# Second sequence's turned row split in another order around the next row's sum, two operand copies on POOL, query tile turned behind the third keys' block

## The chip, the cores and the metric

The kernel runs on one core of a Trainium2 chip. The metric is the device time of one execution in microseconds (us). Engines are named as in the profile: PE multiplies matrices, DVE and ACT do elementwise work, POOL too but only on SBUF, and SP issues DMAs. ACT and POOL also issue DMAs from their own queues. Each engine works through its own instructions in order and waits on semaphores for the others.

## The reference

One encoder layer over two independent sequences of 512 tokens with 1024 features, all in float32:

```python
h = rms_norm(x, ln1)
q, k, v, u, g_att, g_ssm = split(h @ w_in)
y_att = windowed_attention(rms_norm(q), rms_norm(k), v, sink, bias, mask)   # blocks of 128, 3 key blocks each
y_ssm = s5_branch(u, ...)          # state-space scan both ways; y = gelu(y); y * sigmoid(y @ w_glu + b_glu)
mixed = sigmoid(g_att) * y_att + sigmoid(g_ssm) * y_ssm
x = x + mixed @ w_out
h2 = rms_norm(x, ln2)
return x + square(relu(h2 @ w_up)) @ w_down
```

## The kernel before, in words

Every large product is made of three passes. An operand is split into a high part (a cast to the matrix engine's rounded float format, usually by ACT) and a low part (the rest, a subtraction, usually by DVE). `mm3` then multiplies high by high, high by low and low by high. A 128x512 piece that comes out of anything thus costs one cast and one subtraction before it can go into the next product.

The stages run in this order: input projections mixed with the state-space scan, attention, the gated product of the state-space branch, the output projection with the second normalisation, the up projection, and the down projection. In the stretches that matter here the order of PE, ACT and DVE is written out by hand (`tc.manual_schedule`), so their queues hold instructions in program order. Buffers have tags: a new tile under a tag with one buffer waits until every reader of the old tile is done.

**Attention.** Eight steps `i` (four key heads by two sequences, the sequence inside), each with four query blocks `qb`. In one block the kernel computes the scores of the current `Unit` and finishes the previous one (`prev`): its exponentials are turned by PE (`turn`, L983), cast by ACT (`high`, L988) and subtracted by DVE (`low`, L993), for each of its two or three key blocks, and multiplied with the values (`value`, L998). In between PE projects the queries of the next step (`Tile.project`, L913). The query tile of the block before (`rows`) is normalised, turned and split (`Tile.turn`, `high`, `low`, L938 to L949). A `Unit` begins with a small copy on POOL into its column 0 (L962). The last step has no next one. PE then fills in with the first products of the gated stage (`glu_pull`). These need the state-space output `y`, loaded in eight pieces `m` during steps 6 and 7; `split_y` (L1060) casts each half of a piece on ACT at the end of a block, and its subtraction (POOL, L1063) is issued at the start of the next block, from the list `y_lows`. After the loop the last unit is finished, some products are pulled, the reciprocal of the row sums is turned by PE (`final.turn`, L1027), and more products are pulled. All pulls share one list of 96 product steps.

**Output projection.** For each row block `t` (four) and sequence `sq` (two), PE computes the row of 1024 in two halves of 24 matmuls (`out_half`, L1377). DVE adds each half to the residual row `x1`. After the second half ACT squares and sums the row (`power_of`, L1397, into the buffer with tag "xn"), POOL makes the inverse root, DVE scales (`norm_of`, L1409). Between the next row's two halves PE turns this row by eight transposes (`turn_of`, L1425).

The up projection uses a seven-product scheme for blocks of two by two, where the first sequence gives two of the blocks (`B11`, `B21`) and the second two more (`x12`, `x22`). From all four come five operands, `B22`, `T1`, `T2`, `T3`, `T4`. So the turn of a first-sequence row is followed by two splits, and the turn of a second-sequence row by five splits with four differences and two copies between them (L1417 to L1445), through one intermediate `tx` of two halves `tt`, which also has the tag "xn". In the code before, the turn and the splits are issued together, ahead of the next half row:

```python
out_half(x1s[sq], sq, t, b)
if b == halves[0] and owed:
    turn_of(*owed)
```

Then come the store of the finished row to scratch on ACT's queue (L1517), the square and the normalisation. The rows `x1` have two buffers, loaded by SP (L1387). In the last row the raw up weights (`raws`, L1468) are loaded into the buffer of the first half of the output weights, and DVE forms their sums (`up_sums`, L1477); the first up products follow before the last row's turn.

## Time and profile before

| What | us |
|---|---|
| median of 3 runs | 1457.18 |
| lowest, highest run | 1455.81, 1458.38 |
| the profiled execution's own time | 1461.76 |
| its span, first to last instruction | 1460.0 |
| mean granted clock of PE | 0.994 of full |

Times in the profile are microseconds from the span's start. A timeline row gives the start, the length (both us), the engine, the line, the operation, what it writes and reads with their shapes, how many instructions are merged into it, and in brackets the idle time before it and who ended that. PE's rows overlap, since matmuls are pipelined. A row of a table of windows gives the stretch, its length, the busy time of PE, weight loads, DVE, ACT and POOL (with instructions), the granted PE clock, the DMA share and the GB/s.

### The profile page before, as it was taken

Reading aid. Unit: us, or ns where it says so; the run is one execution under the profiler, and the core shown is the slowest. Engines: PE = TensorE matmul, PEld = TensorE weight load, DVE = VectorE, ACT = ScalarE, POOL = GpSimd, SP = SyncE. Lnnn points to the kernel's source line nnn. Section 1 sums busy time; section 2 is a strip of 40 time slices with the busy share of each in tenths; the row PEclk is TensorE's granted clock in tenths of the full one; section 3 lists DMA queues with packets and bytes.
Section 4 is the critical chain, followed back from the end, with each engine's and each line's share of the span. In section 5 each row is a group of like instructions: output and inputs, shape, how many; then the busy total and the mean of one; then the engine's idle time right before and its main releaser. Section 6 shows DMA issues by size and latency. Waiting matters only on the chain.

```text
span 1460.0 us, 22047 instructions
## 1 busy us (share of the span) xinstructions
PE 1442.5 (99%) x7997; PEld 1233.4 (84%) x7997; DVE 1095.2 (75%) x1978; ACT 762.6 (52%) x1361; POOL 243.3 (17%) x394
## 2 busy tenths in 40 slices
PE   9999999999999999999999899999999999999998
PEld 8888888889999999988887688888888888888887
DVE  7999959985458999889964478777776598475654
ACT  8688852234348878883533246445454444333332
POOL 3044452004144432362000000000000000000000
PEclk9999999999999999999999899999999999999999
DMA  7356559539642632445551335444442993454441
GB/s 294 102 176 189 163 162 328 194 106 308 220 144 71 182 107 64 138 151 189 196 181 58 112 106 197 160 148 151 147 144 107 339 334 106 158 187 147 129 130 58
DMA packets 102204, 240.23 MB, mean 165 GB/s; under 512 B 12330, under 2 KB 25130, under 8 KB 102096
## 3 DMA queue, kind: packets, MB, share of 16 engines
q1 hardware_dynamic: 62304, 139.94, 29.5%
q0 software_dynamic: 16320, 48.28, 10.1%
q10 hardware_dynamic: 23472, 50.61, 9.3%
q8 instruction: 63, 1.03, 0.3%
q14 instruction: 45, 0.37, 0.1%
HBM read 169.02 MB, written 81.82 MB: 172 GB/s over the span
## 4 chain that ended last, share of the span: by engine, by line
PE 83%; DVE 9%; issue 4%; ACT 2%; DMA 2%; POOL 1%; ACTq 0%; DVEq 0%; SPq 0%; POOLq 0%
PE bank L119 14%; PE bank L118 14%; PE bank L120 14%; PE acc L187 9%; PE acc L125 5%; PE acc L919 5%; PE po L1002 2%; PE sps L970 2%; PE sps L641 2%; PE tps L986 2%; PE sps L753 2%; DVE t L716 2%; PE acc L118 1%; PE acc L120 1%; PE acc L119 1%
## 5 line engine op out<-in xcount | busy, mean ns | idle before, releaser
L187 PE MATMUL acc<-act,c_hi 128*128 128x512 f32 x768 | 243.8, 395 | 0.0
L119 PE MATMUL bank<-b_lo,a_hi 128*128 128x512 f32 (+1 forms) x449 | 174.4, 389 | 0.0
L120 PE MATMUL bank<-b_hi,a_lo 128*128 128x512 f32 (+1 forms) x449 | 174.4, 389 | 0.0
L118 PE MATMUL bank<-b_hi,a_hi 128*128 128x512 f32 (+1 forms) x449 | 174.4, 389 | 0.0
L187 PEld LDWEIGHTS acc<-act,c_hi 128*128 128x128 f32 x768 | 142.4, 188 | 28.0 <-ACT act L316 0.9
L1654 ACT CAST a_hi<-d_a 128x1024 fp32r<-128x1024 f32 x56 | 59.0, 1054 | 178.0 <-PE bank L119 175.7
L187 PE MATMUL acc<-act,c_lo 128*128 128x512 f32 x384 | 151.4, 394 | 0.0
L118 PE MATMUL bank<-act,act 128*128 128x512 f32 x368 | 143.2, 389 | 0.0
L119 PE MATMUL bank<-act,act 128*128 128x512 f32 x368 | 143.2, 389 | 0.0
L120 PE MATMUL bank<-act,act 128*128 128x512 f32 x368 | 143.2, 389 | 0.0
L1655 DVE TENSOR_TENSOR a_lo<-d_a,a_hi 128x1024 fp32r<-128x1024 f32 x56 | 68.5, 1224 | 98.0 <-ACT a_hi L1654 98.0
L919 PE MATMUL acc<-w_hi,act 128*128 128x256 f32 x512 | 114.1, 291 | 0.1
L120 PEld LDWEIGHTS bank<-b_hi,a_lo 128*128 128x128 f32 x449 | 84.3, 188 | 17.6
L119 PEld LDWEIGHTS bank<-b_lo,a_hi 128*128 128x128 f32 x449 | 84.3, 188 | 17.4
L118 PEld LDWEIGHTS bank<-b_hi,a_hi 128*128 128x128 f32 x449 | 84.3, 188 | 17.3
L919 PEld LDWEIGHTS acc<-w_hi,act 128*128 128x128 f32 x512 | 87.0, 189 | 4.0 <-PE sps L970 0.3
L187 PEld LDWEIGHTS acc<-act,c_lo 128*128 128x128 f32 x384 | 72.2, 188 | 14.8 <-DVE c_lo L178 1.0
L118 PEld LDWEIGHTS bank<-act,act 128*128 128x128 f32 x368 | 69.1, 188 | 14.5
L119 PEld LDWEIGHTS bank<-act,act 128*128 128x128 f32 x368 | 69.1, 188 | 14.4
L120 PEld LDWEIGHTS bank<-act,act 128*128 128x128 f32 x368 | 69.1, 188 | 14.2
L125 PE MATMUL acc<-act,gc_hi 128*128 128x512 f32 x256 | 80.7, 393 | 0.0
L980 ACT ACTIVATE p<-p,nmx 128x257 f32<-128x257 f32 (+1 forms) x128 | 72.0, 563 | 16.1 <-DVE nmx L974 15.2
(358 smaller groups left out, 3439.8 us busy)
## 6 DMA issues: line engine op xcount, KB each, us to landing
d_a<-a_scr SPq DMA_DIRECT2D x56, 512.0 KB, 3.6
raws<-in_w_up_dram SPq DMA_DIRECT2D x32, 512.0 KB, 4.0
a_scr<-t ACTq DMA_DIRECT2D x64, 256.0 KB, 2.9
k<-in_w_down_dram SPq DMA_DIRECT2D x32, 512.0 KB, 6.0
c_raw<-in_w_ug_dram SPq DMA_DIRECT2D x48, 256.0 KB, 4.1
ct_scr<-ctab POOLq DMA_DIRECT2D x16, 512.0 KB, 4.4
ctab_in<-ct_scr POOLq DMA_DIRECT2D x16, 512.0 KB, 6.2
a_scr<-a ACTq DMA_DIRECT2D x32, 256.0 KB, 2.0
```

Of the source, the lines that this page charges most:

```text
L118: PE.matmul(ps, a[0], b[0], start=first, stop=False)
L119: PE.matmul(ps, a[0], b[1], start=False, stop=False)
L120: PE.matmul(ps, a[1], b[0], start=False, stop=last)
L125: PE.matmul(ps, w[wi][:, k, :], rows[yi], start=k + p == 0, stop=k == KT - 1 and p == 2)
L187: PE.matmul(ps, w[wi][:, k, :], hT[s][hi][:, k, :], start=n == 0, stop=n == 3 * KT - 1)
L641: PE.matmul(ps[:, i * P:(i + 1) * P], bm[:, ri, g, :], u_sb[:, gp * SH + g, :], start=True, stop=True)
L716: V.tensor_mul(t1, h[:, i], a8r)
L753: PE.matmul(o, ctab[:, g0 % SI + g, ri, 0:T * CH], st[:, ri, g].rearrange("p s k -> p (s k)"), start=False, stop=ri == 1)
L919: PE.matmul(self.ps, hT[sq][act][:, k, col:col + P], w[:, k % 4, :], start=i == 0, stop=i == 3 * KT - 1)
L980: S.activation(p, p, AF.Exp, bias=self.nmx[:, h:h + 1], scale=-1.0, accum_out=self.sums[:, h, self.qb:self.qb + 1])
L1654: S.copy(hi, src)
L1655: V.tensor_sub(lo, src, hi.bitcast(F32))
```

## The change

There are four edits.

1. In the output projection, `turn_of` is cut in two. The transposes stay where they were; the splits (`put_turned`) are issued behind the second half row. For the second sequence's rows, the same operations are put in another order, with independent ones side by side, and the add and the square of the row that PE has just finished (`last`) stand ahead of the last two subtractions. The store of the finished row is issued behind its normalisation. The very last row keeps the old order. The first two raw up weights are loaded one row earlier.
2. In `split_y`, the casts of piece 6 are copies on POOL, issued directly ahead of its subtractions.
3. From the seventh attention step on (`i` above 5), the third key block of the previous unit is turned and split ahead of the query tile.
4. Behind the last unit 13 products are pulled instead of 10.

```diff
         def split_y(m, half):
-            S.copy(hi, lo.bitcast(F32))
-            return lambda: GP.tensor_tensor(lo, lo.bitcast(F32), hi.bitcast(F32), op=ALU.subtract)
+            def low():
+                if m == 6:
+                    GP.tensor_copy(hi, lo.bitcast(F32))
+                GP.tensor_tensor(lo, lo.bitcast(F32), hi.bitcast(F32), op=ALU.subtract)
+            if m != 6:
+                S.copy(hi, lo.bitcast(F32))
+            return low
...
                     cur.largest(3)
+                    if n3 > 2 and i > 5:
+                        prev.turn(2)
                     if rows:
                         rows.turn()
-                    if n3 > 2:
+                    if n3 > 2 and i < 6:
                         prev.turn(2)
...
                     project(4)
+                    if n3 > 2 and i > 5:
+                        prev.high(2)
+                        prev.low(2)
                     if rows:
                         rows.high()
                         rows.low()
-                    if n3 > 2:
+                    if n3 > 2 and i < 6:
                         prev.high(2)
                         prev.low(2)
...
-            glu_pull(10)
+            glu_pull(13)
             gate_out(1)
             final.invert()
             final.turn()
...
+        def put_turned(sq, t, last=lambda: None, between=()):
...
             if sq == 0:
                 xb.reverse()
                 put(B11, xb[0])
                 put(B21, xb[1])
+                last()
                 return
             tx = rn2.tile([P, 2, 4, P], F32, tag="xn", name="tx", bufs=1)
             tt = [tx[:, 0], tx[:, 1]]
             x11, x21, x12, x22 = xb
+            if not between:
+                S.copy(tt[0], x11)
+                high(B22, x22)
+                V.tensor_sub(tt[0], x12, tt[0])
+                low(B22, x22)
+                high(T1, tt[0])
+                V.tensor_sub(tt[1], x22, tt[0])
+                low(T1, tt[0])
+                high(T2, tt[1])
+                S.copy(tt[0], x22)
+                low(T2, tt[1])
+                V.tensor_sub(tt[0], tt[0], x12)
+                high(T3, tt[0])
+                V.tensor_sub(tt[1], tt[1], x21)
+                high(T4, tt[1])
+                last()
+                low(T3, tt[0])
+                low(T4, tt[1])
+                xb.clear()
+                return
...
         for t in range(NT // 2):
+            if t == 1:
+                w_first = [load_part(0, i) for i in range(2)]
...
             for sq in range(NSEQ):
-                halves = (0, 1) if t else (1,)
-                for b in halves:
...
-                    out_half(x1s[sq], sq, t, b)
-                    if b == halves[0] and owed:
-                        turn_of(*owed)
-                if t == 3 and sq == 1:
+                x1, tail = x1s[sq], (sq, t) == (1, 3)
+                if t:
+                    out_half(x1, sq, t, 0)()
+                    turn_of(*owed)
+                    if tail:
+                        put_turned(*owed[:2])
...
+                add = out_half(x1, sq, t, 1)
+                scaled = []
+
+                def add_and_square():
+                    add()
+                    scaled.extend(power_of(x1))
+
+                if t and not tail:
+                    put_turned(*owed[:2], last=add_and_square)
+                else:
+                    add_and_square()
+                if tail:
                     break
-                S.dma_start(x1_scr[rows_of(sq, t), :], x1s[sq])
-                owed = sq, t, norm_of(x1s[sq], *power_of(x1s[sq]))
-        scaled = power_of(x1s[1])
+                if owed and not t:
+                    turn_of(*owed)
+                    put_turned(*owed[:2])
+                owed = sq, t, norm_of(x1, *scaled)
+                S.dma_start(x1_scr[rows_of(sq, t), :], x1)
...
-        turn_of(1, 3, xn, [lambda: None, lows[0], lambda: next(second), lows[1]])
+        turn_of(1, 3, xn)
+        put_turned(1, 3, between=[lambda: None, lows[0], lambda: next(second), lows[1]])
```

`out_half` now returns its add as a function to be called later; the other helpers are unchanged.

## The prediction

> **What bounds the kernel now.** I read the page's busy line first, then the table of who waited for whom, limited to the matrix engine, then the timeline around its longest waits, then the windows there for the granted clock.

> ```profile
> PE 1442.5 (99%) x7997; PEld 1233.4 (84%) x7997; DVE 1095.2 (75%) x1978; ACT 762.6 (52%) x1361; POOL 243.3 (17%) x394
> ...
> PE tps L1425 <- DVE rn_xn L1409: 9.0, 3, 3.0
> PE po L1002 <- ACT ph L990: 1.2, 3, 0.8
> ...
> PE tps L1027 <- DVE rsum L1022: 0.4, 1, 0.4
> ```

> PE sets the end almost everywhere, so only an instant at which PE stands still can be won. The change removes no matmul. The waits (total, times, longest) name three places, and the change touches all three. The large one is three waits of 3.0 us for a normalised row at the turning transposes (L1425), in the output-projection stage.

> ```profile
> 763.45 1.03 PE L1425 MATMUL sps<-ident,rn_xn 128*128 128x128 f32 x8
> ...
> 764.56 0.40 PE L119 MATMUL acc<-act,act 128*128 128x512 f32 x1
> ...
> 774.99 0.39 PE L120 MATMUL acc<-act,act 128*128 128x512 f32 x1
> 778.38 1.94 PE L1425 MATMUL tps<-ident,rn_xn 128*128 128x128 f32 x8 [3.00 <-DVE rn_xn L1409]
> ...
> 793.02 1.04 PE L1425 MATMUL sps<-ident,rn_xn 128*128 128x128 f32 x8
> ...
> 821.43 1.03 PE L1425 MATMUL sps<-ident,rn_xn 128*128 128x128 f32 x8
> ...
> 853.72 1.04 PE L1425 MATMUL sps<-ident,rn_xn 128*128 128x128 f32 x8
> ```

> A wait costs more than its 3.0 us. From 764.56 to 774.99 lie 46 matmul steps: 10.43/46 = 0.2267 us each. One turn costs 764.56 - 0.23 - 763.45 = 0.88. Between the second sequence's turns at 763.45 and 793.02 PE has four half rows of 24 matmuls and two turns: 96 x 0.2267 + 2 x 0.88 = 23.53. It took 29.57, so 6.04 are lost. From 793.02 to 821.43 the work is the same and 28.41 - 23.53 = 4.88 are lost. From 821.43 to 853.72 there are 108 matmuls (three half rows and 36 of the first up products), 26.25 us of work, so 6.04 are lost again. **Sum 16.96 us**, of which the standing still is 778.38 - (774.99 + 0.23) = 3.16 each, 9.48. The rest is the clock:

> ```profile
> 778.00:779.00 1.00, 0.62 (x3) 0.65 (x4) 0.84 (x2) 0.00 (x0) 0.00 (x0) 0.50 0.00 0
> ...
> 784.00:785.00 1.00, 1.00 (x5) 0.84 (x4) 0.00 (x0) 0.00 (x0) 0.00 (x0) 0.85 0.00 0
> ...
> 645.00:650.00 5.00, 4.25 (x22) 3.18 (x21) 3.05 (x7) 4.68 (x13) 5.00 (x5) 1.00 0.40 105
> ```

> The column after POOL's is the granted clock: 0.50 when PE resumes, 0.85 only in the stretch from 784. The short wait at 646 (below) leaves it at 1.00.

> **The row order, step by step.** Why is the row late? The first sequence's row is added, squared and normalised only after the second sequence's whole five-part split:

> ```profile
> 764.58 0.59 ACT L1417 CAST act<-sps 128x512 fp32r<-128x512 f32 x1 [4.27 <-PE sps L1425]
> ...
> 765.06 0.59 ACT L1437 COPY tx<-tps 128x512 f32<-128x512 f32 x1
> ...
> 765.80 0.68 DVE L1438 TENSOR_TENSOR tx<-sps,tx 128x512 f32<-128x512 f32 x1
> ...
> 766.52 0.62 ACT L1417 CAST act<-tx 128x512 fp32r<-128x512 f32 x1 [0.87 <-DVE tx L1438]
> ...
> 767.17 0.69 DVE L1419 TENSOR_TENSOR act<-tx,act 128x512 fp32r<-128x512 f32 x1 [0.69 <-ACT act L1417]
> ...
> 773.11 0.69 DVE L1419 TENSOR_TENSOR t<-tx,t 128x512 fp32r<-128x512 f32 x1 [0.69 <-ACT t L1417]
> 773.72 0.68 DVE L1383 TENSOR_TENSOR x<-acc,x 128x512 f32<-128x512 f32 x1
> 774.43 0.33 ACTq L1517 DMA_DIRECT2D x_scr<-x  x1
> 774.81 1.06 ACT L1400 ACTIVATE rn_xn<-x 128x1024 f32<-128x1024 f32 x1 [1.73 <-DVE x L1383]
> ...
> 776.95 1.28 DVE L1409 SCALAR_TENSOR_TENSOR rn_xn<-x,rs,ln_bc 128x1024 f32<-128x1024 f32 x1 [2.55 <-POOL rs L1403]
> ```

> The split runs from 764.58 to the add at 773.72 because each part waits on the one before, alternating between ACT and DVE. The hops, start to start: ACT to DVE 0.65 (766.52 to 767.17), DVE to ACT 0.72 (765.80 to 766.52), DVE to DVE 0.61 (773.11 to 773.72), ACT to ACT 0.48 (764.58 to 765.06). The new order issues the same seven ACT and nine DVE operations, with the independent ones in between. Walked with these hops from 764.58 = 0: ACT copy 0, ACT B22 0.48; DVE x12 difference 0.65, B22 rest 1.26; ACT T1 1.37; DVE x22 difference 1.87, T1 rest 2.48; ACT T2 2.59, ACT copy (it overwrites what the T1 rest reads) 3.20; DVE T2 rest 3.24, difference 3.85, last difference 4.46; ACT T3 4.57, T4 5.18. The add is free at 5.07 but waits for its half row: 763.45 + 0.88 + 24 x 0.2267 + 0.16 of pipeline = 769.93, that is 5.39 with a small hop. Then the rests of T3 at 6.00 and T4 at 6.61.

> The square writes into the one buffer (tag "xn") that the split's intermediate occupies, and the rest of T4 is its last reader. So I let the square wait for that rest, not for the add: 6.61 + 0.72 = 7.33, or 771.91. From square to transposes stays 778.38 - 774.81 = 3.57, giving 775.48 against PE's 775.22: **0.26 us left of each wait**. If the square needed only the add (5.39 + 0.72 + 3.57, or 774.26), nothing would be left. Both ends give the same sum within 0.8. A stand of 0.26 is shorter than that at 646, which left the clock whole, so I let the clock loss go too: 16.96 - 0.78 = **16.2 us**.

> The row's store to scratch moves behind the normalisation, so its 0.4 us of ACT queue (774.43 to 774.81) leaves the chain. What is late then is the release of the row's buffer:

> ```profile
> 778.27 0.33 SPq L1387 DMA_DIRECT2D x<-in_x_dram  x1
> ...
> x_scr<-x ACTq DMA_DIRECT2D x2, 512.0 KB, 2.7
> ```

> The next load goes out at 778.27, when the normalisation ends. Afterwards it waits for the later of that (771.91 + 3.42 = 775.3) and the store's landing (771.91 + 1.5 + 2.7 = 776.1). Still earlier than now, and the row is added only at the half row ending at 793.02: nothing. The two early weight loads go out on SP's queue a row sooner; their first user is an ACT cast two rows later, so nothing. In the very first rows one square moves ahead of two casts on ACT, at most 1.06 us (its length), behind a half row of PE work: nothing.

> **The tail.** What follows the third wait had that wait as cover. The raw up weights reuse the output weights' buffer, so their load starts where PE's last use ends, and the sums of them stand on DVE ahead of the last row's add:

> ```profile
> 840.17 0.68 DVE L1477 TENSOR_TENSOR held<-raws 128x512 f32<-128x512 f32 x1
> ...
> DMA to landing us min/median/max: 3.5/4.5/8.3
> ```

> The third turn started at 836.36 (the same 3.00 us wait) and the sums 3.81 later. Without the wait they want the data near 837.0. The loads go out from 833.4 and land 3.5 to 8.3 us later, so DVE waits between 0 and 4.7 us; by the median 0.9. Behind it stand the last add, square and normalisation, about 4.1 us (0.72 + 2.14 + 1.28). PE comes to that row only 36 matmuls (8.2 us) after the add's half row, so about 4 us of cover remain. I take nothing.

> **The attention edits.**

> ```profile
> 642.92 2.18 ACT L1062 CAST act<-act 128x512 fp32r<-128x512 f32 x4
> 645.64 0.59 ACT L990 CAST ph<-tps 128x512 fp32r<-128x512 f32 x1
> ...
> 646.28 0.50 PE L1002 MATMUL po<-ph,va 128*128 128x512 f32 x1 [0.75 <-ACT ph L990]
> ...
> 643.62 5.04 POOL L1063 TENSOR_TENSOR act<-act,act 128x512 fp32r<-128x512 f32 x4 [2.53 <-ACT act L1062]
> 649.85 0.21 POOL L962 COPY p<-vec 128x4 f32<-128x4 f32 x1
> 651.59 2.55 POOL L1063 TENSOR_TENSOR act<-act,act 128x512 fp32r<-128x512 f32 x2 [1.52 <-ACT act L1062]
> ...
> 654.23 0.71 PE L125 MATMUL acc<-act,gc_hi 128*128 128x512 f32 x2
> ...
> L888 POOL COPY kd<-kn x8: 603/613/616, 426.3 to 603.5; 128x512 f32<-128x512 f32 x8
> ```

> Two of the four ACT casts (m = 6) leave: 1.09 us, more than PE's 0.75 wait behind them. **Gain 0.75.** They become POOL copies of c each. No row shows POOL casting to fp32r. The nearest are its one-input copy of that size, 0.61, and its two-input subtraction, 2.55/2 = 1.28; I take 0.61, the same number of inputs. POOL is in order: its column copy would end at 650.06 + 2c, then the m = 7 rests, 2.55 more, end at 652.61 + 2c = 653.83. The matmul that reads them is the second at 654.23, some 0.3 in, now 0.75 earlier: about 653.8. I charge 0.2. At c = 1.28 it is 1.4, at c = 0.48 nothing.

> ```profile
> 622.07 0.40 PE L1002 MATMUL po<-ph,va 128*128 128x512 f32 x1
> 622.58 0.50 PE L1002 MATMUL po<-pl,va 128*128 128x512 f32 x1
> ...
> 663.75 0.39 PE L125 MATMUL acc<-act,gc_lo 128*128 128x512 f32 x1
> 664.50 0.27 PE L1027 MATMUL tps<-ident,rsum 128*16 128x128 f32 x1 [0.36 <-DVE rsum L1022]
> ```

> (The 663.75 row is the last product before the row-sum transpose.) Turning the third block ahead of the query tile acts only in the seventh step, on two units: the second product comes 0.51 after the first instead of 0.23. **Gain 0.28.** The query half is delayed by one ACT and one DVE operation and is read a step later. Three more products before the transpose are 0.68 of work over a gap of 664.50 - 663.75 - 0.23. **Gain 0.52.** The total of products stays.

> **Sum.** 16.2 + 0.75 - 0.2 + 0.28 + 0.52 = 17.5 us. The profiled execution took 1461.76 (span 1460.0 and 1.76 around it); the median of the runs is 4.6 below it. 1457.18 - 17.5 = **1439.7**; a profiled execution would be near 1444.2.

> **Rivals.** (A) The clock does not fall in the timed executions. For it: they are 4.6 us shorter than the profiled one, and the standing still is only just long enough. Against: all three falls show here. Then only 9.48 - 0.78 + 1.35 = 10.1 is won: 1447.1. [...]

> (B) The new order's hops are longer than those of the old, about 1 us a row, PE stands 1.2 us without a clock fall: 3 less, 1442.7. For: the walk uses each engine back to back. Against: 1 us is more than any single hop of the fence above, and no operation is added.

> (C) The up weights land late, near 8.3: the last row is 0.7 late after its cover and its first split pushes PE too, 2 us: 1441.7.

> (D) The change does not do what it says: the split keeps its length, since the ACT-DVE alternation bounds it, and only the store's 0.4 and the add's 0.6 leave. The stand falls to 2.2 and the clock falls still: 3 + 1.35, 1452.8.

> (E) Slower: the two POOL copies. POOL's queue holds the rests and the last unit's column behind them, and PE's products need them. The stall is 2c - 1.0; it eats everything from c = 9.3 on, and a copy of 10 us gives 1458.4. Against: the two nearest rows, quoted above, are 0.61 and 1.28.

> **Numbers.** Forecast 0.66 (own range 1437.5 to 1442), A 0.12, B 0.10, C 0.05, D 0.04, E 0.03. The range takes the forecast, B, C and reaches A: 1437 to 1447.2. A measurement of this kernel tells about 0.2%, 2.9 us, from no change. All but E, and a sliver of D, are faster: 0.95, same 0.03, slower 0.02.

> **What would show it.** Right: no wait of PE at the turns over 0.5, granted clock 1.00 from 775 to 840, the second sequence's turns 23.8 apart, the add before the last two rests on DVE, the square starting after the rest of T4. Wrong: PE waits above 1 us there, a clock of 0.50, DVE waiting for raw weights until the last turn is late, PE waiting for the m = 7 rests.

## The result and the profile after

| Kernel | median of the runs (range) | share of the time before (95% interval) | profiled execution | its clock |
|---|---|---|---|---|
| before | 1457.18 (1455.31 to 1459.96, 5 runs) | 1 | 1461.76 | 0.994 |
| after | 1444.94 (1444.66 to 1445.92, 5 runs) | 0.9916 (0.9902 to 0.9931) | 1445.04 | 1.0 |

The change is faster by 12.2 us. The time is inside the range, 5.2 us above the forecast of 1439.7. The pair of profiled executions lies 16.7 apart.

The page of the kernel after, its first lines:

```profile
span 1443.3 us, 22044 instructions
...
PE 1435.6 (99%) x7997; PEld 1228.0 (85%) x7997; DVE 1094.9 (76%) x1978; ACT 762.3 (53%) x1359; POOL 244.1 (17%) x396
```

Each of these engines has as many instructions as before, but for the two casts that went from ACT to POOL. Now the waits of the kernel after from 610 to 845 us, those of PE first and those of the weight loads (PEld) behind them: who waited for whom, total, times, longest. The three waits of 3.0 us at the turns are gone from PE. What remains of them stands at the weight loads, 1.4 us for all three.

```profile
PE po L1002 <- ACT ph L990: 0.4, 2, 0.2
PE acc L125 <- POOL act L1066: 0.3, 1, 0.3
...
PEld tps L1432 <- DVE rn_xn L1424: 1.4, 3, 0.5
...
PEld acc L125 <- ACT ga L825: 0.4, 1, 0.4
```

The timeline of PE after, the second sequence's turns:

```profile
762.74 1.03 PE L1432 MATMUL sps<-ident,rn_xn 128*128 128x128 f32 x8
...
786.54 1.03 PE L1432 MATMUL sps<-ident,rn_xn 128*128 128x128 f32 x8
...
810.39 1.03 PE L1432 MATMUL sps<-ident,rn_xn 128*128 128x128 f32 x8
...
837.00 1.03 PE L1432 MATMUL sps<-ident,rn_xn 128*128 128x128 f32 x8
```

They are 23.80, 23.85 and 26.61 apart, against 29.57, 28.41 and 32.29 before: 16.01 us less. The work alone takes 23.53, 23.53 and 26.25, so 0.95 of the 16.96 is left. The clock over the whole stage, in the window's column after POOL's:

```profile
757.00:850.00 93.00, 92.86 (x439) 76.72 (x437) 56.70 (x84) 37.96 (x68) 5.55 (x14) 1.00 0.32 112
```

The timeline of DVE and ACT after, in the first of these rows:

```profile
769.27 0.69 DVE L1395 TENSOR_TENSOR x<-acc,x 128x512 f32<-128x512 f32 x1 [0.37 <-PE acc L120]
769.88 0.68 DVE L1443 TENSOR_TENSOR act<-tx,act 128x512 fp32r<-128x512 f32 x1
770.48 0.69 DVE L1443 TENSOR_TENSOR t<-tx,t 128x512 fp32r<-128x512 f32 x1
771.20 1.06 ACT L1415 ACTIVATE rn_xn<-x 128x1024 f32<-128x1024 f32 x1 [1.64 <-DVE t L1443]
```

The add (769.27) waits for its half row, then come the rests of T3 and T4, then the square, 0.72 after the last rest. The square starts 3.61 us earlier than before (771.20 against 774.81); counted from the turn ahead of it (762.74 and 763.45) 2.90 of that is left, which is what the row order gives.

**The attention part** gained little. I measure it from the first row-sum transpose of step 7 (L1027) to the first turn; the kernel before has 612.66 and 757.12 there, 144.46 us:

```profile
612.66 0.27 PE L1027 MATMUL tps<-ident,rsum 128*16 128x128 f32 x1
...
757.12 1.03 PE L1425 MATMUL tps<-ident,rn_xn 128*128 128x128 f32 x8
```

and after 143.79, 0.67 less:

```profile
612.62 0.27 PE L1027 MATMUL tps<-ident,rsum 128*16 128x128 f32 x1
...
756.41 1.03 PE L1432 MATMUL tps<-ident,rn_xn 128*128 128x128 f32 x8
```

16.01 and 0.67 make 16.68 of the 16.72 by which the profiled executions differ. So the trace is accounted for, and the question is why the medians are only 12.2 apart.

### The profile page after: what moved, and what is told of

It is laid out like the page before. It is cut to its first block, busy times and chain, and to the rows that moved or that the text cites. A ratio compares the mean times of both kernels' runs of the same rounds, so it can differ in the third digit from the quotient of the medians.

```text
span 1443.3 us, 22044 instructions
## 1 busy us (share of the span) xinstructions
PE 1435.6 (99%) x7997; PEld 1228.0 (85%) x7997; DVE 1094.9 (76%) x1978; ACT 762.3 (53%) x1359; POOL 244.1 (17%) x396
## 3 DMA queue, kind: packets, MB, share of 16 engines
q8 instruction: 63, 1.03, 0.3%
## 4 chain that ended last, share of the span: by engine, by line
PE 84%; DVE 8%; issue 4%; DMA 2%; ACT 1%; POOL 1%; DVEq 0%; SPq 0%; ACTq 0%; POOLq 0%
PE bank L118 14%; PE bank L120 14%; PE bank L119 14%; PE acc L187 9%; PE acc L125 6%; PE acc L919 5%; PE po L1002 2%; PE sps L970 2%; PE sps L641 2%; PE tps L986 2%; PE sps L753 2%; PE acc L120 2%; PE acc L119 2%; PE acc L118 2%; DVE t L716 2%
## 5 line engine op out<-in xcount | busy, mean ns | idle before, releaser
L119 PE MATMUL bank<-b_lo,a_hi 128*128 128x512 f32 (+1 forms) x449 | 174.4, 389 | 0.0
L120 PE MATMUL bank<-b_hi,a_lo 128*128 128x512 f32 (+1 forms) x449 | 174.4, 389 | 0.0
L119 PE MATMUL bank<-act,act 128*128 128x512 f32 x368 | 143.2, 389 | 0.0
L120 PE MATMUL bank<-act,act 128*128 128x512 f32 x368 | 143.2, 389 | 0.0
L119 PEld LDWEIGHTS bank<-b_lo,a_hi 128*128 128x128 f32 x449 | 84.3, 188 | 17.5
L120 PEld LDWEIGHTS bank<-b_hi,a_lo 128*128 128x128 f32 x449 | 84.3, 188 | 17.5
L125 PE MATMUL acc<-act,gc_hi 128*128 128x512 f32 x256 | 81.2, 394 | 0.3 <-POOL act L1066 0.3
L120 PEld LDWEIGHTS bank<-act,act 128*128 128x128 f32 x368 | 69.1, 188 | 14.3
L119 PEld LDWEIGHTS bank<-act,act 128*128 128x128 f32 x368 | 69.1, 188 | 14.2
## 6 DMA issues: line engine op xcount, KB each, us to landing
d_a<-a_scr SPq DMA_DIRECT2D x56, 512.0 KB, 3.6
raws<-in_w_up_dram SPq DMA_DIRECT2D x32, 512.0 KB, 4.0
k<-in_w_down_dram SPq DMA_DIRECT2D x32, 512.0 KB, 5.6
ct_scr<-ctab POOLq DMA_DIRECT2D x16, 512.0 KB, 4.8
ctab_in<-ct_scr POOLq DMA_DIRECT2D x16, 512.0 KB, 6.4
```

The costliest lines, as they stand in the source:

```text
L119: PE.matmul(ps, a[0], b[1], start=False, stop=False)
L120: PE.matmul(ps, a[1], b[0], start=False, stop=last)
L125: PE.matmul(ps, w[wi][:, k, :], rows[yi], start=k + p == 0, stop=k == KT - 1 and p == 2)
```

## The experiments

Two measures are used. The time of a whole execution does not tell differences below about half a microsecond, so single terms are read from the trace: the attention interval above, and the distances of the turns.

### Where 4.5 us of the profiled gain went: the clock

Theory W: in the runs of before the clock falls after only some of the stands (a stand is a stretch in which PE stands still ahead of a turn). Theory P: the profiled execution of before is longer for another reason.

**The row order alone**, edit 1 of the diff above put on the kernel before:

```diff
+        def put_turned(sq, t, last=lambda: None, between=()):
...
+                if t and not tail:
+                    put_turned(*owed[:2], last=add_and_square)
```

Expected:

> The kernel before with the first edit alone (the row order of the output projection); attention as before. Two theories of why the timed gain (12.24 us) is smaller than that between the two profiled executions (16.72). W: in timed executions of the kernel before the clock falls after only some of the three stands of 3.16 us. P: the profiled execution of before was slower by some 4.6 us for another reason, somewhere else. Both expect this kernel near 1445.6 (median of before less 12.24, plus the 0.7 that the attention edits gave in the profiled pair), the turns of the second sequence 23.8 apart and a clock of 1.00. By the prediction's own terms (1.35 for attention) it would be 1446.3 with the clock as W has it, 1441 without W.

**The attention edits alone**, 2 to 4, on the kernel before:

```diff
+                    GP.tensor_copy(hi, lo.bitcast(F32))
...
+                    if n3 > 2 and i > 5:
+                        prev.turn(2)
...
+            glu_pull(13)
```

Expected:

> The kernel before with edits 2, 3 and 4 alone (POOL copies of piece 6, third block ahead of the query tile, 13 products); rows as before. By the prediction 1.35 us faster in the place of the first turn on PE (763.45 would become 762.1). By the trace of the changed kernel 0.7 only (762.74): the third block's 0.28 is given back at once, because DVE is busy throughout there and is late at the next low part; the m = 7 rests cost 0.45 and not 0.2. The three stands stay, so the time of the whole, 1456.5 by the trace, is blurred by the clock of each execution.

Edit 1 alone took 1445.90 (1445.52 to 1446.09), 0.9913 of before (0.9901 to 0.9926): all of the gain that a whole time can show. Its clock was 0.999 to 1.0. Its turns are 23.80, 23.88 and 26.59 apart, its attention interval is 144.45, as before. The attention edits alone took 1459.50 (1454.52 to 1461.78), where 1456.5 was expected, 1.0003 (0.9993 to 1.0014) of before; their interval is 143.80, so 0.66 is there and is lost in a spread of 7 us from run to run.

That spread is mostly the clock. Over the 41 runs of before that were timed beside the experiments the time went from 1454.75 to 1462.51 with a mean granted clock from 0.999 down to 0.994. A line through them falls by 1.1 us for each 0.001 (correlation -0.86) and stands at 1454.5 for a clock of 1.000. The profiled execution (1461.76 at 0.994) is near the bad end; less the 7.48 of clock that its own trace shows it would be 1454.3, which is the line's value. The median of the 41 runs, 1458.41, is 1.2 above that of the five in the table, so the gain is 12 to 13.5 us, by which runs are taken.

**A longer and a shorter stand**, both on the kernel before. The longer one repeats the last low part of each second-sequence split twice more, into the same place:

```diff
+            if not between:
+                for _ in range(2):
+                    V.tensor_sub(T4[1][:, :, cs], tt[1], T4[0][:, :, cs].bitcast(F32))
```

Expected:

> The kernel before with the last low part of each second-sequence split (but the last row's) computed three times instead of once: 2 x 0.6 us more on DVE, so each stand of PE grows from 3.16 to about 4.37. W: now the clock falls every time in every execution: 3 x 1.2 of standing and the clock loss that timed executions had escaped (about 5 us) come on top, 1457.2 + 3.6 + 5 = 1465.8, and the executions differ less than those of before. P: 3.6 more and nothing else, 1460.8.

The shorter one issues the store of the row behind its normalisation, and nothing else:

```diff
-                S.dma_start(x1_scr[rows_of(sq, t), :], x1s[sq])
                 owed = sq, t, norm_of(x1s[sq], *power_of(x1s[sq]))
+                S.dma_start(x1_scr[rows_of(sq, t), :], x1s[sq])
```

Expected:

> The kernel before with only the store of the finished row moved behind its normalisation, so each stand of PE shrinks from 3.16 to about 2.78. W: the clock hardly falls: 3 x 0.38 of standing and most of the timed clock loss (about 2.9) go, 1453.2, granted clock above 0.998 in most executions. P: 1.1 less, 1456.0.

The longer stand (waits of 4.45) took 1465.47 (1463.84 to 1467.14), 1.0049 (1.0036 to 1.0062), with a clock of 0.993 to 0.994 in all five runs: W's 1465.8, not P's 1460.8. (The stands grew by 1.45 each and not by 1.2, which adds 0.7 to both numbers.) The windows of the kernel with the longer stand (the clock is the third number from the end):

```profile
778.50:785.00 6.50, 4.73 (x16) 4.09 (x17) 3.18 (x4) 1.07 (x2) 0.30 (x1) 0.50 0.23 81
...
809.25:815.75 6.50, 4.91 (x16) 4.27 (x17) 3.17 (x4) 1.07 (x2) 0.12 (x1) 0.50 0.23 81
...
840.00:846.50 6.50, 5.03 (x16) 4.38 (x17) 4.29 (x6) 1.07 (x2) 0.01 (x1) 0.50 0.96 354
```

Three times 6.5 us and more at half clock. The windows of the kernel before show one that is half as long, at the second stand:

```profile
777.50:784.00 6.50, 5.62 (x18) 4.78 (x19) 2.63 (x4) 1.07 (x2) 0.00 (x0) 0.50 0.24 81
...
808.25:811.50 3.25, 3.25 (x13) 2.87 (x11) 1.32 (x3) 1.07 (x2) 0.00 (x0) 0.50 0.50 161
...
835.50:842.00 6.50, 5.64 (x18) 4.80 (x19) 4.32 (x7) 1.07 (x2) 0.00 (x0) 0.50 0.84 291
```

These windows also show W in runs that have no trace. One stretch of 3.4 us at half clock (808.20 to 811.61 in the kernel before) takes 0.0012 off the mean clock of 1460 us; the profiled execution, with five such lengths, is at 0.994. Three of the 41 runs are at 0.999, which leaves room for one such stretch at most, so at least two of their three stands passed without a fall.

The shorter stand (waits of 2.64 to 2.72) took 1456.24 (1454.16 to 1459.70), 0.9982 (0.9973 to 0.9992). I expected the falls to vanish and 1453.2; that failed. Less time goes to half clock, but not none: the mean granted clock of these runs is 0.9975 on average, against 0.9963 in the 23 runs of before beside them. The time lies at P's number, 1456.0, but that does not speak for P: here too it goes with the clock, from 1454.2 at 0.999 to 1459.7 at 0.996. The windows of the kernel with the shorter stand:

```profile
778.50:781.50 3.00, 3.00 (x11) 2.41 (x9) 1.29 (x2) 1.07 (x2) 0.00 (x0) 0.50 0.53 175
...
806.00:809.00 3.00, 3.00 (x12) 2.71 (x13) 0.86 (x2) 1.07 (x2) 0.00 (x0) 0.50 0.50 175
...
830.00:840.00 10.00, 7.28 (x37) 5.86 (x36) 5.88 (x9) 2.23 (x4) 0.79 (x2) 1.00 0.78 263
```

and the timeline of its PE, two of its turns:

```profile
805.87 1.94 PE L1425 MATMUL tps<-ident,rn_xn 128*128 128x128 f32 x8 [2.70 <-DVE rn_xn L1409]
...
833.87 1.06 PE L1425 MATMUL tps<-ident,rn_xn 128*128 128x128 f32 x8 [2.72 <-DVE rn_xn L1409]
```

Two stands of the same length in one execution: the clock falls at one (eight transposes take 1.94) and not at the other (1.06). So the length of a stand does not decide alone. W holds; what decides besides the length is in the last section.

### The attention edits one by one

The kernel after again, with no edit, as the control. Expected:

> The changed kernel itself, as the yardstick of this group: 1444.9, and executions that lie within about 1 us of each other, because no stand of PE is long enough for the clock to fall in any of them.

Without edit 3 (the third block is turned and split behind the query tile again):

```diff
-                    if n3 > 2 and i > 5:
+                    if n3 > 2 and i > 50:
                         prev.turn(2)
...
-                    if n3 > 2 and i < 6:
+                    if n3 > 2 and i < 60:
                         prev.turn(2)
...
```

Expected:

> The changed kernel with edit 3 undone (query tile turned ahead of the third key block, as before). By the prediction 0.28 slower. By the trace, DVE has no idle time in these two blocks, so PE's 0.28 is handed on to the next low part and the kernel is as fast as with the edit: within 0.1.

Without edit 2 (the casts of piece 6 on ACT again):

```diff
-                if m == 6:
-                    GP.tensor_copy(hi, lo.bitcast(F32))
...
-            if m != 6:
-                S.copy(hi, lo.bitcast(F32))
...
+            S.copy(hi, lo.bitcast(F32))
...
```

Expected:

> The changed kernel with edit 2 undone (the casts of piece 6 on ACT, as before). By the prediction 0.75 - 0.2 = 0.55 slower. By the trace of the changed kernel the value product comes 0.92 earlier by matmul starts and 0.45 is lost at the m = 7 rests, so 0.47 slower, 1445.4; PE's 0.75 wait for the cast returns and its 0.29 wait for POOL goes.

Without edit 4:

```diff
-            glu_pull(13)
+            glu_pull(10)
```

Expected:

> The kernel after without edit 4 (ten gate products ahead of the last output block again, not thirteen). Same interval of the trace, 143.79 to 143.86 with edit 4. If edit 4 buys the 0.52 us at the row-sum transpose and gives 0.29 back 21 us later, where the weight load waits for ScalarE's activation: the wait of 0.36 before the transpose is back, the later wait of 0.44 is gone, and the interval is 144.05. If the later wait has nothing to do with edit 4 (it stays): 144.35. If edit 4 is worth nothing: 143.8.

| Kernel | median (range) | share of before | attention interval |
|---|---|---|---|
| after, again | 1445.41 (1445.05 to 1446.47) | 0.9917 (0.9903 to 0.9930) | 143.84 |
| without edit 3 | 1445.47 (1444.60 to 1446.34) | 0.9916 (0.9903 to 0.9930) | 143.83 |
| without edit 2 | 1445.59 (1444.70 to 1446.05) | 0.9916 (0.9902 to 0.9929) | 144.34 |
| without edit 4 | 1444.80 (1444.36 to 1444.99) | 0.9908 (0.9893 to 0.9923) | 144.01 |

The times cannot tell them apart; the interval can, since two runs of one kernel agree in it within 0.05 (143.79 and 143.84, mean 143.82). Edit 2 is worth 0.52, edit 3 nothing, edit 4 0.19. The timeline of the kernel after around edit 2:

```profile
645.31 0.39 PE L1002 MATMUL po<-ph,va 128*128 128x512 f32 x1
...
646.07 0.61 POOL L1065 CAST act<-act 128x512 fp32r<-128x512 f32 x1
...
649.95 1.29 POOL L786 TENSOR_TENSOR gc_lo<-c_raw,gc_hi 128x512 fp32r<-128x512 f32 x1
...
651.33 2.55 POOL L1066 TENSOR_TENSOR act<-act,act 128x512 fp32r<-128x512 f32 x2
...
653.93 0.50 PE L125 MATMUL acc<-act,gc_hi 128*128 128x512 f32 x1 [0.29 <-POOL act L1066]
```

Counted from the row-sum transpose, the value product starts 0.93 earlier than before (645.31 less 612.62, against 646.28 less 612.66), with no wait ahead of it, and the product behind it 1.04 earlier, since it follows after 0.23 and not after 0.34. Then PE waits 0.29 for the rests of m=7, which stand on POOL behind a subtraction of gate weights (649.95) that is already in the queue; the matmuls behind that wait have lost about half of the gain.

Edit 3 takes the wait ahead of the second product at 622 away, and pays it back in the next block. The timeline of PE of the kernel after:

```profile
622.02 0.40 PE L1002 MATMUL po<-ph,va 128*128 128x512 f32 x1
622.26 0.40 PE L1002 MATMUL po<-pl,va 128*128 128x512 f32 x1
...
625.26 0.47 PE L1002 MATMUL po<-ph,va 128*128 128x512 f32 x1
626.30 0.50 PE L1002 MATMUL po<-pl,va 128*128 128x512 f32 x1
```

0.24 from product to product at 622 (0.51 before), but 1.04 at 625 (0.71 before: 625.70 to 626.41). DVE is busy for 9.62 of the 10 us from 620 to 630 in the kernel before, and its operation of L1051 starts at 629.62 in both traces: the step goes at DVE's pace.

Edit 4 takes the wait at the row-sum transpose away, and part of it comes back 21 us later. The timeline of ACT and of the weight loads of the kernel after:

```profile
684.81 0.68 ACT L825 ACTIVATE ga<-acc,vec 128x512 f32<-128x512 f32 x1
...
685.55 0.30 PEld L125 LDWEIGHTS acc<-act,gc_hi 128*128 128x128 f32 x2 [0.44 <-ACT ga L825]
```

The next product wants the accumulator that this activation reads, and ACT is held by DVE's products of the gate: its cast at 683.76, ahead of this activation, waits 3.09 for them. PE's matmuls there start 0.29 late in all (0.41 and 0.57 between rows in place of 0.23 and 0.46). In the timeline of the kernel without edit 4 this wait is gone and the old one is back:

```profile
663.43 0.27 PE L1027 MATMUL tps<-ident,rsum 128*16 128x128 f32 x1 [0.36 <-DVE rsum L1022]
```

So 0.52 is won and 0.29 given back, as expected of this run (144.05; 144.01 came).

**The wait that edit 2 leaves.** The remainder of the gate weights is put behind the rests of m=7:

```diff
...
-                    if lower:
-                        lower()
-                        lower = None
+                    if lowers and (i, qb) != (7, 2):
+                        while lowers:
+                            lowers.pop(0)()
...
```

Expected:

> The kernel after, with the remainder of the last block of gate weights (1.29 us on POOL) put behind the remainders of the operand tile m=7 instead of ahead of them. The term to be settled is the 0.45 us that TensorE loses there after the change (a wait of 0.29 for POOL and a slow start). Measured in the trace, from the first transpose of the row sums in step 7 to the first turn of a second-sequence row: 143.79 to 143.86 in the runs of the kernel after so far. Theory H: the wait goes and nothing takes its place: 143.4. Rival: TensorE comes 0.45 earlier to the gate products, whose accumulators VectorE and ScalarE free no sooner (a wait of 0.44 of the weight load for ScalarE's activation of line 825 stands there in the kernel after): 143.8, and that wait grows to about 0.9.

(The expectation names the turn of a second-sequence row; its numbers are those of the interval used here, to the first turn.) Interval 143.28, so 0.54 won; time 1444.34 (1444.26 to 1445.80), 0.9907 (0.9891 to 0.9923). The wait downstream grew by 0.03 only, to 0.47. The rival falls: counted from the first row-sum transpose, ACT's activation of line 825 starts 0.52 earlier too (685.53 less 613.86, against 684.81 less 612.62).

### The 0.26 left of each wait, and the tail

**A buffer of its own for the square's throw-away output**, so that the square needs the add alone:

```diff
-            S.activation(xn, x1, AF.Square, scale=D ** -0.5, accum_out=ss)
+            junk = rn2.tile([P, D], mybir.dt.bfloat16, tag="junk", name="junk", bufs=1)
+            S.activation(junk, x1, AF.Square, scale=D ** -0.5, accum_out=ss)
...
```

(For its space one of the three buffers of the early raw weights goes.) Expected:

> The changed kernel, with the square's throw-away output in a buffer of its own (bfloat16; the sum beside it and the normalised row are computed as before), so that the square need not wait for the rest of T4. Theory of the prediction: the square waits for the buffer; it would start 1.2 us earlier (add start + 0.7 and not T4 rest + 0.7), and the 0.27, 0.32 and 0.36 us that are left of the three waits go: 1444.0, turns 23.53 apart. Rival: the square waits for the add only and what is left of the wait has another cause (POOL's root, DVE's normalisation): no change, 1444.9, turns 23.80 apart.

The turns are 23.58 and 23.55 apart: the rest was the wait for T4's last reader. But the time is 1446.18 (1445.26 to 1446.53), 0.9920 (0.9907 to 0.9932), no better, because the third period grew to 27.71. The timeline of PE and DVE of this kernel:

```profile
809.52 1.03 PE L1433 MATMUL sps<-ident,rn_xn 128*128 128x128 f32 x8
...
828.99 0.69 DVE L1522 TENSOR_TENSOR held<-raws 128x512 f32<-128x512 f32 x1 [4.72 <-DMA raws<-in_w_up_dram]
...
831.53 0.68 DVE L1395 TENSOR_TENSOR x<-acc,x 128x512 f32<-128x512 f32 x1
...
834.10 0.50 PE L118 MATMUL acc<-act,act 128*128 128x512 f32 x1 [0.87 <-ACT act L1530]
...
837.23 1.03 PE L1433 MATMUL sps<-ident,rn_xn 128*128 128x128 f32 x8
```

The sums of the raw up weights wait 4.72 us for their load. Behind them on DVE stands the last row's add, behind it on ACT the square, and behind that the cast for which PE waits. Of the 2.42 by which this wait is longer than in the kernel after (2.30, shown below) half is DVE, which is free 1.2 earlier; the other half is the load. It goes out 0.9 earlier (821.49 against 822.39), and yet the sums start 1.24 later (828.99 against 827.75). The median from issue to landing, in the kernel after and in this one:

```profile
raws<-in_w_up_dram SPq DMA_DIRECT2D x5, 512.0 KB, 5.0
...
raws<-in_w_up_dram SPq DMA_DIRECT2D x5, 512.0 KB, 7.1
```

Why the load takes longer here no run shows.

**The add ahead of the sums**, on the kernel with that buffer:

```diff
                         load_up(1)
-                        up_sums(0, range(4))
...
                 if tail:
+                    up_sums(0, range(4))
                     break
...
```

Expected:

> The kernel with the square's throw-away output in a buffer of its own (turns 23.58 and 23.55 us apart, but 27.71 for the third period), with the four sums of raw up weights on VectorE put behind the last row's second add instead of ahead of it. Theory: in the tail the add is held only by the sums ahead of it in VectorE's order, which wait 4.72 us for the raw up weights. With the add first it starts at about 828.1 (its products end then) and not at 831.5, the wait of 0.87 before the first of the second up products is gone, the third period is 26.3 to 26.6, and the kernel is about 1.2 us shorter than with the buffer alone (profiled span about 1442.3, time about 1445.0). Rival: the raw up weights themselves hold the cast of that product: a wait of 0.5 or more of TensorE for ScalarE stays there, the third period is 27.2 or more, and the time that with the buffer alone.

The timeline of PE and DVE of this kernel:

```profile
809.31 1.03 PE L1433 MATMUL sps<-ident,rn_xn 128*128 128x128 f32 x8
...
827.61 0.69 DVE L1395 TENSOR_TENSOR x<-acc,x 128x512 f32<-128x512 f32 x1 [3.55 <-PE acc L120]
828.86 0.69 DVE L1522 TENSOR_TENSOR held<-raws 128x512 f32<-128x512 f32 x1 [0.56 <-DMA raws<-in_w_up_dram]
...
832.85 0.39 PE L118 MATMUL acc<-act,act 128*128 128x512 f32 x1
...
835.58 1.03 PE L1433 MATMUL sps<-ident,rn_xn 128*128 128x128 f32 x8
```

The add starts at 827.61 instead of 831.53, the sums wait only 0.56, PE does not wait, and the third period is 26.27, the work alone. The load lands no earlier (828.86 for the sums); it only no longer holds up the add. Time 1444.09 (1443.64 to 1445.04), 0.9905 (0.9889 to 0.9920).

**All three together**: this kernel with the late gate remainder, whose diff stands above. Expected:

> The kernel with its own buffer for the square and the add ahead of the sums, and in the attention part the remainder of the last gate block behind those of m=7: the candidate for a version faster than both. If both theories hold: turns 23.6 apart, third period 26.3 to 26.6, the interval of the trace in the attention part 143.4, and in all 1.5 to 1.7 us off the kernel after: time about 1443.8 against 1445.4. If both rivals hold: 1445.9.

The interval is 143.21, the turns are 23.55, 23.55 and 26.26 apart, and the time is 1443.65 (1443.44 to 1444.80), 0.9903 (0.9885 to 0.9920). That is the best version: by the trace 1.5 us better than the kernel after (0.6 in the attention part, 0.9 at the turns), and about as much by the medians (1444.94 and 1445.41 against 1443.65), whose ranges overlap only around 1444.7. From the kernel without the late gate remainder (1444.09) the times do not tell it apart; the interval does (143.21 against 143.76).

## Why the prediction was right, and where it was wrong

- **The loss at the turns, right for the execution it was read from.** 16.2 was to be won of 16.96; 16.01 was. The walk of the new order holds: the add ahead of the last two rests, the square 0.72 after the rest of T4. Counted from the turn, it was put at 8.46 (771.91 less 763.45) and came at 8.46 (771.20 less 762.74). That number rests on the half row and the last hops alone: DVE is idle for 0.37 ahead of the add (0.32 predicted), so the walk before it had that much slack. Turns 23.8 apart were predicted, 23.80 and 23.85 came.
- **The step that failed: "1457.18 - 17.5".** The 7.48 of clock in the sum were read from a profiled execution of 1461.76 and taken off the median of other executions. Rival A had the reason half right. That the stand is only just long enough was an estimate of its author; of the shorter stands two fell (waits of 2.64 and 2.70) and one did not (2.72). The falls do happen in the timed runs, but not as many: by the line through the 41 runs the execution at 1457.18 loses 1457.18 - 1454.5 = 2.7 to the clock. With that term: 9.48 - 0.95 + 2.7 + 0.67 = 11.9 against 12.2 measured. Taken from the profiled execution itself, the sum was good: 1444.2 predicted, 1445.04 measured. Since the changed kernel has no falls, its profiled execution and its median are the same, and 1444.2 was the number to forecast. The time is inside the stated range only because that reaches to rival A at 1447.1. The forecast's own range, 1437.5 to 1442, misses it, and 1444.94 is nearer to A than to the forecast.
- **Attention, 1.35 predicted, 0.67 measured.** Edit 2 net 0.55 predicted, 0.52 measured, with POOL's copy at 0.61 as taken. That the net fits is luck in part, since two misses cancel: the products came 0.93 to 1.04 earlier (0.75 predicted), and the rests of m=7 took 0.54 of it back (0.2 predicted), as the run with the late gate remainder shows. POOL ends these rests where the walk put it (653.83 predicted, 651.33 + 2.55 = 653.88 measured); PE is there sooner than was taken. "Gain 0.28" for edit 3 failed: nothing, since DVE sets the pace of that step. "Gain 0.52" for edit 4 was there at its place and lost 0.29 at the next accumulator; 0.19 to 0.22 remain.
- **The tail, "I take nothing", right, but with less cover than written.** DVE waits there for the raw weights in the kernel after too, 2.30 (0.9 by median, 4.7 at most predicted). The timeline of DVE, ACT and PE of the kernel after:

```profile
827.75 0.69 DVE L1521 TENSOR_TENSOR held<-raws 128x512 f32<-128x512 f32 x1 [2.30 <-DMA raws<-in_w_up_dram]
...
830.29 0.68 DVE L1395 TENSOR_TENSOR x<-acc,x 128x512 f32<-128x512 f32 x1
...
832.12 1.13 ACT L1529 CAST act<-raws 128x512 fp32r<-128x512 f32 x2
...
834.28 0.39 PE L118 MATMUL acc<-act,act 128*128 128x512 f32 x1
```

  The first cast ends about 0.6 after 832.12 and PE starts at 834.28: some 1.5 of cover, not 4. Rival C's transfer became the bound in the kernel with the buffer, where DVE was free another 1.2 earlier and the load landed 1.2 later, though its victim is this cast and not the last row's turn.
- **Rivals B, D and E** fell: the hops are those of the old order, the stand is gone, and the POOL copy takes 0.61.

## What to carry to other kernels

When a loss depends on the state of the clock, read it from the same executions against which it is taken off: list clock and time of every run, and forecast the changed kernel from the profiled execution if the change removes the cause. A gain at one instant of the bounding engine is worth what the next shared resource leaves of it (the next accumulator, the engine that paces the step, the load behind it; edit 4 kept 0.19 of its 0.52), so follow it one buffer further. In a queue that is worked through in order, as DVE's was here (the add started at 831.53 behind the sums and at 827.61 ahead of them), put what the bounding engine needs next ahead of work that waits for a transfer.

## What the runs showed of the hardware that was not expected

```profile
808.00:808.25 0.25, 0.25 (x3) 0.25 (x4) 0.25 (x1) 0.00 (x0) 0.00 (x0) 0.90 0.00 0
...
835.50:835.75 0.25, 0.00 (x0) 0.00 (x0) 0.25 (x1) 0.00 (x0) 0.00 (x0) 0.51 1.29 164
```

The distances are 30.72 and 27.31, nine and eight steps of 3.413 us, and the same step fits the falls of the three other traces with stands: 776.10, 806.82 and 834.13 with the attention edits alone, 778.43, 809.15 and 839.87 with the longer stand, 778.42 and 805.73 with the shorter one. Each stretch at half clock lasts one or two steps (808.20 to 811.61 and 777.48 to 784.3 in the kernel before). I laid the grid over the twelve stands of these four traces; a stand is counted from 0.23 after the start of the last matmul to the start of the next. The clock fell in the eleven cases where PE stood still for 2.13 us or more of one step (2.7 and 2.8 in the shorter stands that fell), and not in the one where no step had more than 2.04: the third of the shorter stands, 830.99 to 833.87, which a step of the grid at 833.03 (the fall at 805.73 and eight steps) splits into 2.04 and 0.84. It stayed low for a second step where PE stood still for 0.84 or more of that step, and rose where it was 0.14 or less. So in these traces a stand of about 3 us cost its length, and on top of it nothing (the third of the shorter stands), 1.72 us (4.88 less 3.16, the second stand of the kernel before) or 2.88 (6.04 less 3.16, its other two), by where it fell on the grid; by the steps it would be 1.7 (half of one) and 3.0 (half of what is left of two when PE resumes). The phase differs between the four traces: from the last matmul ahead of the first of these stands to the first fall it is 2.49 in the kernel before (777.48 less 774.99), 2.36 with the attention edits alone, 3.00 with the longer stand and 3.68 with the shorter one. That it differs in the same way among the 41 runs of before, and so makes their spread, is the reading that fits; it was not shown run by run, since only the profiled ones have a trace.
